# Up projection of the gated MLP as seven float16 block products per weight pair and 1,024 tokens, gated values through DRAM

## The chip, the cores and the metric

The kernel runs on one core of a Trainium2 chip. The core has TensorE (PE, matrix products out of SBUF into PSUM), VectorE (DVE), ScalarE (ACT) and GpSimd (POOL) for work by element, and SyncE (SP), which here only issues DMA transfers between DRAM and SBUF. The metric is the device time of one execution in microseconds. Each engine runs its own list of instructions in order; semaphores make one list wait for another.

## The reference

One layer of a diffusion block over 2,048 latent tokens of width 1,024 (and 256 context tokens, which only feed keys, values and states). First a mixer of attention and gated DeltaNet heads, then an output projection with a gated residual, then the part that is changed here:

```python
def conv_ffn(h, w_up, conv_w, conv_b, w_down):
    """Gated MLP with a centred depthwise conv between up-projection and activation."""
    u = depthwise_conv(h @ w_up, conv_w) + conv_b      # w_up (1024, 2*2816), conv over 3 tokens
    gate, val = jnp.split(u, 2, axis=-1)
    return (jax.nn.silu(gate) * val) @ w_down          # w_down (2816, 1024)
...
x = x + g1 * lat_out
x = x + g2 * conv_ffn(modulate(x, norm2_g[l], sh2, sc2), w_up[l], ffn_conv_w[l], ffn_conv_b[l], w_down[l])
return rms_norm(x, final_norm_g)
```

## The kernel before

Tokens lie along the free axis, features along the 128 partitions. D = 1024 makes KT = 8 tiles of 128 input features; the 2,816 hidden features make NJ = 22 pairs of a gate tile and a value tile; the 2,048 tokens make NCH = 4 blocks of 512.

The layer's earlier stages (projections, attention and the DeltaNet scan) and the output projection (`output`) are ordered by a list scheduler (`Plan`), which writes each engine's list from costs and priorities. All of the MLP behind it is issued in the order in which the code is written (`manual_schedule`).

Every product keeps about float32 accuracy by splitting each operand into a rounded part and the rest (float32r, "hi" and "lo") and adding three matmuls: hi by hi, hi by lo, lo by hi (`prods`, lines 520 to 522).

The MLP runs token block by token block. For each block there are 44 "up" units (one feature tile each, 8 x 3 = 24 matmuls of 128x512 into one PSUM bank `pu`), followed by 24 "down" units (8 output tiles `pdn`, each summed over 22 hidden tiles in parts of 8, 8 and 6). A unit's weights (`raw`, 2 buffers, 512 KB) are fetched by SP, rounded by ACT (`leading`, line 1703) and their rest taken by DVE (`rest`, line 1708) into `ws` (3 buffers), two units ahead; so up weights are loaded and split four times, once for each block. Behind an up unit `after_up` copies `pu` to SBUF (`ue`, line 1734), applies the three taps of the convolution on DVE (`cv`, lines 1742 and 1745), and after each value tile takes SiLU, multiplies, and splits the result into `hid`, which stays in SBUF: 22 tiles of hi and lo. Two tokens of each row are carried to the next block (`carry`).

The normalised input of the next block (`h2`) is read back from DRAM (`h2c`) and split while the down units run, one tile for each output tile (line 1842 ff.), and the final norm of a block (`last_norm`) is spread over the next block's up units.

Of the kernel before, what the change touches and what calls it, by code (L numbers as in the profile page):

```python
# [40 lines left out]
VTOP = 1024.0  # L41
GTOP, ROWV, SC = 2048.0, 4096.0, 1024.0
# [378 lines left out]
def kernel(  # L421
# [22 lines left out]
    h2c = dram.tile([NCH, P, KT, 512], F32, name="h2c")  # L444
    hcd = dram.tile([P, 2, KT, TC], F32, name="hcd")
# [1073 lines left out]
    hp3 = p3.enter_context(tc.tile_pool(name="hp3", bufs=1, side="right", reuse_waits="tile"))  # L1519

    def load_h2(pool, tag, bufs, tb):
        h2 = hp3.tile([P, 2, KT, 512], F32R, tag="h2", name=f"h2_{tb}")
        for k in range(KT):
            raw = pool.tile([P, 512], F32, tag=tag, name=f"h2raw_{tb}_{k}", bufs=bufs)
            SY.dma_start(out=raw, in_=h2c[tb, :, k, :])
            S.copy(out=h2[:, 0, k, :], in_=raw)
            V.tensor_tensor(out=h2[:, 1, k, :], in0=raw, in1=h2[:, 0, k, :].bitcast(F32), op=ALU.subtract)
        return h2

    def output(plan, x3, s3, ol3):  # L1530
# [50 lines left out]
        def normed(xv, tb):  # L1581
            acc = mk(s3, [P, 512], F32, "nacc", f"nacc_b{tb}", 2)
            S.activation(out=acc, in_=xv[:, 0, :], func=AF.Square)
            for k in range(1, KT):
# [3 lines left out]
            yield  # L1588
            ps = mk(psn, [P, 512], F32, "nps", f"nps_b{tb}", 1)
            for j in range(4):  # L1590
                PE.matmul(out=ps[:, 2 * j:2 * j + 2], lhsT=acc[:, j * P:(j + 1) * P], rhs=ones[:, 0:2], start=True,
                          stop=True)
            rs = rep_rstd(plan, psn, "nps", 1, s3, 2, ps, 512, f"b{tb}")
            for k in range(KT):
                V.scalar_tensor_tensor(out=xv[:, k, :], in0=xv[:, k, :], scalar=aff2[:, k:k + 1], in1=rs,
                                       op0=ALU.mult, op1=ALU.mult)
                S.activation(out=xv[:, k, :], in_=xv[:, k, :], func=AF.Identity, bias=mod2[:, 8 + k:9 + k])
                if k % 2:
                    SY.dma_start(out=h2_l[tb][:, k - 1:k + 1, :], in_=xv[:, k - 1:k + 1, :])
# [3 lines left out]
        h2 = None  # L1603
# [313 lines left out]
```

## Time and profile before

| | |
|---|---|
| median of 3 runs | 3490.8 us (3486.12 to 3490.93) |
| span of the profiled execution (no other time is given for it) | 3482.1 us |
| around the span, median less span | 8.7 us |
| MLP, from the first `pu` to the end | 3482.1 - 1995.6 = 1486.5 us |
| bytes from and to HBM, whole span | 306.17 and 88.11 MB |
| busy DVE, ACT and POOL, whole span | 66%, 48%, 41% |

The profile is one execution. A row of a group gives line, engine, operation, `out<-in` with shapes, count, busy us, mean ns of one, and then the time its engine sat idle before it and what ended that. A row of stages gives the busy time of each engine in a stretch of the span. In a timeline a row has start, duration, engine, line and names; an idle stretch before it stands in brackets with what ended it. PE rows overlap: a matmul of 512 columns is shown as 0.39 us long, while the next starts 0.23 us after it, so the pace is read from starts.

### The profile page before, as it was taken

The page shows a single profiled execution, that of the slowest core. Times are in us where ns is not written, and L with a number is a line of the kernel's source. Part 1 is how long each engine was busy: PE and PEld are TensorE (multiplying, and loading weights), DVE is VectorE, ACT ScalarE, POOL GpSimd, SP SyncE. Part 2 cuts the span into 40 slices and gives each one's busy share as a digit, 9 for nine tenths or more (in the row PEclk, how much of TensorE's full clock was granted, in tenths as well). Part 3 has the DMA queues.
Part 4 walks back from the last instruction along what each step waited for, and adds up shares of the span by engine and source line. Part 5 has one row for each costly group of instructions (what it writes and reads, how often), then busy time and mean ns, then how long its engine had stood idle before and what let it go on. Part 6 is the DMA issues. An engine that isn't in the chain of part 4 may idle for free.

```text
span 3482.1 us, 64968 instructions
## 1 busy us (share of the span) xinstructions
PE 3309.7 (95%) x26025; PEld 2692.3 (77%) x26025; DVE 2312.2 (66%) x3601; ACT 1661.9 (48%) x2600; POOL 1432.9 (41%) x1429
## 2 busy tenths in 40 slices
PE   6799999979999999999878999999999999999998
PEld 3799888857777777777556778888888888888898
DVE  5665577878777789888656577636773577447743
ACT  5443243457877777767644443323332333223331
POOL 5685455557777777778855411000110011001100
PEclk8899999999999999999989999999999999999999
DMA  6323335641222233222156733343334333433332
GB/s 232 88 66 96 123 114 147 190 136 56 79 86 92 67 110 91 90 88 74 41 176 211 241 119 97 101 135 103 116 96 133 110 117 96 123 118 116 97 108 92
DMA packets 218527, 398.09 MB, mean 114 GB/s; under 512 B 21496, under 2 KB 96856, under 8 KB 217952
## 3 DMA queue, kind: packets, MB, share of 16 engines
q1 hardware_dynamic: 216272, 388.52, 35.3%
q0 software_dynamic: 1952, 5.42, 0.6%
q8 instruction: 204, 3.34, 0.4%
q14 instruction: 99, 0.81, 0.1%
HBM read 306.17 MB, written 88.11 MB: 113 GB/s over the span
## 4 chain that ended last, share of the span: by engine, by line
PE 73%; DVE 10%; POOL 6%; DMA 4%; issue 3%; ACT 3%; SPq 0%; POOLq 0%; DVEq 0%; ACTq 0%
PE pu L521 9%; PE pu L522 9%; PE pu L520 9%; PE sc L403 6%; PE ops L403 5%; PE pdn L522 5%; PE pdn L521 5%; PE pdn L520 5%; PE po L403 3%; PE sm L403 2%; PE pa L403 1%; DVE mx L403 1%; PE pg L522 1%; PE pg L521 1%; PE pg L520 1%
## 5 line engine op out<-in xcount | busy, mean ns | idle before, releaser
L403 POOL TENSOR_TENSOR lp<-p,hp 128x1024 f16<-128x1024 f32 x288 | 623.3, 2172 | 212.2 <-DVE hp L403 66.9
L520 PE MATMUL pu<-h,ws_u 128*128 128x512 f32 x1408 | 550.8, 391 | 3.2 <-ACT h L403 3.2
L521 PE MATMUL pu<-h,ws_u 128*128 128x512 f32 x1408 | 549.3, 390 | 2.3 <-DVE h L403 2.3
L522 PE MATMUL pu<-h,ws_u 128*128 128x512 f32 x1408 | 548.9, 390 | 0.0
L1736 POOL COPY carry<-ue 128x2 f32<-128x2 f32 x132 | 25.2, 191 | 892.6 <-ACT ue L1734 892.6
L403 DVE TENSOR_REDUCE mx<-sm 128x1 f32<-128x512 f32 x512 | 336.6, 683 | 65.3 <-PE sm L403 63.7
L403 ACT ACTIVATE p<-sc 128x1024 f32<-128x1024 f32 x288 | 295.3, 1025 | 139.5 <-PE sc L403 128.2
L520 PEld LDWEIGHTS pu<-h,ws_u 128*128 128x128 f32 x1408 | 264.9, 188 | 60.2 <-ACT h L403 4.6
L521 PEld LDWEIGHTS pu<-h,ws_u 128*128 128x128 f32 x1408 | 264.9, 188 | 59.7 <-DVE h L403 4.0
L522 PE MATMUL pdn<-hid,ws_d 128*128 128x512 f32 (+2 forms) x880 | 307.4, 349 | 0.0
L521 PE MATMUL pdn<-hid,ws_d 128*128 128x512 f32 (+2 forms) x880 | 307.4, 349 | 0.0
L522 PEld LDWEIGHTS pu<-h,ws_u 128*128 128x128 f32 x1408 | 264.9, 188 | 54.6
L520 PE MATMUL pdn<-hid,ws_d 128*128 128x512 f32 (+2 forms) x880 | 306.4, 348 | 0.0
L1734 ACT COPY ue<-pu 128x512 f32<-128x512 f32 x176 | 103.4, 587 | 368.8 <-PE pu L522 367.4
L1745 DVE SCALAR_TENSOR_TENSOR cv<-ue,cols,cv 128x512 f32<-128x512 f32 (+1 forms) x352 | 265.0, 753 | 15.5
L1708 DVE TENSOR_TENSOR ws_u<-raw_u,ws_u 128x1024 fp32r<-128x1024 f32 x176 | 214.6, 1219 | 18.0 <-ACT ws_u L1703 18.0
L403 PE MATMUL sc<-q,kh 128*128 128x512 f16 x576 | 219.2, 381 | 4.9 <-ACT p L403 3.8
L1742 DVE TENSOR_SCALAR cv<-ue,cols 128x512 f32<-128x512 f32 (+1 forms) x176 | 96.4, 548 | 189.9 <-ACT ue L1734 185.4
L403 PE MATMUL sc<-qx,kx 128*128 128x512 f16 x576 | 219.1, 380 | 0.0
L1733 POOL COPY ue<-carry 128x2 f32<-128x2 f32 x176 | 95.6, 543 | 291.3 <-DVE cv L1745 291.2
L1708 DVE TENSOR_TENSOR ws_d<-raw_d,ws_d 128x1024 fp32r<-128x1024 f32 (+1 forms) x96 | 109.1, 1136 | 157.4 <-ACT ws_d L1703 155.2
L403 ACT CAST hp<-p 128x1024 f16<-128x1024 f32 x192 | 201.1, 1048 | 3.6
(586 smaller groups left out, 8070.5 us busy)
## 6 DMA issues: line engine op xcount, KB each, us to landing
raw_u<-in_wu SPq DMA_DIRECT2D x176, 512.0 KB
raw_d<-in_wd SPq DMA_DIRECT2D x64, 512.0 KB
tk<-gsc SPq DMA_DIRECT2D x34, 512.0 KB
tT<-gsc SPq DMA_DIRECT2D x66, 256.0 KB
wm<-in_wm SPq DMA_DIRECT2D x64, 256.0 KB
gsc<-kd SPq DMA_DIRECT2D x64, 256.0 KB
raw_o<-in_wo SPq DMA_DIRECT2D x32, 512.0 KB
raw_d<-in_wd SPq DMA_DIRECT2D x32, 384.0 KB
```

The source lines that it names most:

```text
L403: fn(**{k: v.get() if isinstance(v, Lazy) else v for k, v in kw.items()})
L520: PE.matmul(out=ps, lhsT=hi_l(k), rhs=hi_r(k), start=st, stop=False)
L521: PE.matmul(out=ps, lhsT=hi_l(k), rhs=lo_r(k), start=False, stop=False)
L522: PE.matmul(out=ps, lhsT=lo_l(k), rhs=hi_r(k), start=False, stop=en)
L1708: V.tensor_tensor(out=made[u][:, 1, :n], in0=raws[u][:, :n], in1=made[u][:, 0, :n].bitcast(F32), op=ALU.subtract)
L1733: G.tensor_copy(out=ue[:, 0:2], in_=carry[:, b, :])
L1734: S.copy(out=ue[:, 2:514], in_=ps)
L1736: G.tensor_copy(out=carry[:, b, :], in_=ue[:, 512:514])
L1742: V.tensor_scalar(out=cv[:, :W], in0=ue[:, 0:W], scalar1=fw[0], scalar2=cols[:, C_FB + b:C_FB + b + 1], op0=ALU.mult, op1=ALU.add)
L1745: V.scalar_tensor_tensor(out=cv[:, :W], in0=ue[:, i:i + W], scalar=fw[i], in1=cv[:, :W], op0=ALU.mult, op1=ALU.add)
```

## The change

**What is computed.** A pair (gate tile, value tile) of up weights is a 2 x 2 matrix of blocks: rows gate and value, columns the first and second 512 input features (A11, A12; A21, A22). The activations of 1,024 tokens are one too: rows the halves of the features, columns two token blocks (B11, B12; B21, B22). Their product has four results. Before, it takes eight block products of 4 x 3 = 12 matmuls each; the change takes seven (`P1` to `P7`, Strassen's scheme in Winograd's form) from sums of weights (S1 to S4) and of activations (T1 to T4), and adds the products up in PSUM and on DVE.

**Parts.** The parts are float16 (hi and lo, three matmuls as before) instead of float32r. So that they fit, activations are scaled by one bound from the modulation (`scale_h2`), weights by each pair's root mean square (`prep`: two ACT squares with accumulators, a small PE matmul `uns` that sums over partitions, a POOL power), and the convolution's taps are scaled back (`fw`).

**Order.** The up projection of all tokens now comes first, 22 pairs x 2 halves of the tokens = 44 steps; the weights of a pair are fetched and made once (`fetch_up`, `prep`: 7 ACT casts, 7 POOL subtractions, 4 DVE sums), spread over the two steps of the pair before. Each step works its own P1, P6, P5, P2, P7 and, between P6 and P5, the P4 and P3 of the step before. The blocks of the first 1,024 tokens are made inside the output projection (`early`), those of the second during the first steps (`late_blocks`), where the last token block's norm now also lies (`norm_tail`).

**Gated values** are written to DRAM (`hidc`) at the end of `after`, and the down units of each block read them back and split them (`load_part`, parts of 8, 8 and 6 tiles, through 3 buffers `hraw`; for the first block partly through 2 buffers inside the last up step). Parts 0 and 1 share the two buffers of `ol3`, part 2 has one; so part i of the next block can be filled only once part i of this one has been used for the last time. The final norm of a block (`last_norm`) now follows behind the next block's first down units.

```diff
+    hidc = dram.tile([NJ, P, T + 2], F32, name="hidc")
...
+    BLK = ("B11", "T2", "T1", "B21", "T3", "T4", "B22")
+    def split(hi_e, lo_e, dst, src):
...
+            hi_e.copy(out=dst[0], in_=src)
...
+        lo_e.tensor_tensor(out=dst[1], in0=src, in1=dst[0], op=ALU.subtract)
+    def prep(e, raw, j, junk_tag, s_tag):
+        g, v = raw
...
+        for r, t in enumerate((g, v)):
...
+            e.S.activation(out=junk, in_=t, func=AF.Square, accum_out=ss[:, r:r + 1])
+            yield
+        ps = e.tile(pt3, [P, 512], F32, "pt", f"uns_{j}", 2)
+        e.PE.matmul(out=ps[:, 0:2], lhsT=ones, rhs=ss, start=True, stop=True)
+        e.V.tensor_reduce(out=sg[:, 0:1], in_=ps[:, 0:2], axis=AX, op=ALU.add)
...
+        e.G.tensor_tensor(out=sg[:, 0:1], in0=sg[:, 0:1], in1=mhalf, op=ALU.pow)
+        yield
...
+        for t in (g, v):
+            e.S.activation(out=t, in_=t, func=AF.Copy, scale=sg[:, 0:1])
+            yield
...
+        def put(n, x):
+            split(e.S, e.G, [at[n][:, f] for f in range(2)], x)
+        e.V.tensor_tensor(out=s, in0=a21, in1=a22, op=ALU.add)
+        put("A11", a11)
+        yield
+        put("S1", s)
+        yield
+        e.V.tensor_tensor(out=s, in0=s, in1=a11, op=ALU.subtract)
+        e.V.tensor_tensor(out=a21, in0=a11, in1=a21, op=ALU.subtract)
+        put("S2", s)
...
+        e.V.tensor_tensor(out=a12, in0=a12, in1=s, op=ALU.subtract)
+        put("A22", a22)
+        yield
+        put("S4", a12)
+        yield
...
+        def product(ps, w, b, first):
+            for k in range(4):
+                for f, (x, y) in enumerate(((0, 0), (0, 1), (1, 0))):
+                    PE.matmul(out=ps, lhsT=w[:, x, k, :], rhs=b[:, y, k, :], start=first and k + f == 0,
+                              stop=k == 3 and f == 2, skip_group_check=True)
...
+        def P6(s):
+            s.bb = bank(s, "ub")
+            product(s.bb, s.w["S2"], s.b["T2"], True)
+            s.u2 = half(s, "u2", "nsq", 2)
+            V.tensor_tensor(out=s.u2, in0=s.bb, in1=s.s1, op=ALU.add)
...
+        def P7(s):
+            product(s.bb, s.w["S3"], s.b["T3"], False)
...
+            V.tensor_tensor(out=u3, in0=s.bb, in1=s.s1, op=ALU.add)
+            V.tensor_tensor(out=s.ev[:, 514:1026], in0=s.c, in1=u3, op=ALU.add)
+        def P4(s):
+            product(s.bb, s.w["A22"], s.b["T4"], False)
+            V.tensor_tensor(out=s.ev[:, 2:514], in0=s.bb, in1=s.s1, op=ALU.add)
...
+        def after(s):
+            W, cv = s.W, []
+            for r, t in enumerate((s.eg, s.ev)):
...
+                S.activation(out=c, in_=t[:, 0:W], func=AF.Identity, scale=s.fw[:, 3 * r:3 * r + 1],
+                             bias=cols[:, C_FB + b:C_FB + b + 1])
+                for i in (1, 2):
+                    V.scalar_tensor_tensor(out=c, in0=t[:, i:i + W], scalar=s.fw[:, 3 * r + i:3 * r + i + 1],
+                                           in1=c, op0=ALU.mult, op1=ALU.add)
...
+                yield
+            S.activation(out=cv[0], in_=cv[0], func=AF.Silu)
+            V.tensor_tensor(out=cv[1], in0=cv[0], in1=cv[1], op=ALU.mult)
+            SY.dma_start(out=hidc[s.j, :, 1024 * s.sb:1024 * s.sb + W], in_=cv[1])
+            yield
...
-        units += [("u", tb, b, 0, KT) for b in range(2 * NJ)]
-        units += [("d", tb, cb, a, n) for cb in range(KT) for a, n in parts]
+    units = [(tb, cb, a, n) for tb in range(NCH) for cb in range(KT) for a, n in parts]
...
+        def prepared(j):
+            yield from prep(direct, raw_u.pop(j), j, "nacc", "nacc")
+            if j + 1 < NJ:
+                raw_u[j + 1] = fetch_up(direct, j + 1)
...
+            elif sb == 0 and n >= 4 and j + 1 < NJ:
+                work = prepared(j + 1)
+            if final:
+                work = chained(load_part(0, 0, ol3.tile([P, 2, KT, OLW], F32R, tag="ol", name="hid_0_0"), s3, "ndg", 2))
+            for i, f in enumerate((P1, P6, P4, P3, P5, P2, P7)):
+                if f in (P4, P3):
+                    if prev:
+                        f(prev)
+                        if f is P3:
+                            post = after(prev)
+                else:
+                    f(s)
+                next(post, None)
...
+                next(extra, None)
+                next(work, None)
...
+    def load_part(tb, i, at, pool, tag, bufs):
...
+            SY.dma_start(out=raw, in_=hidc[a + k, :, 512 * tb:512 * tb + W])
+            S.copy(out=at[:, 0, k, :W], in_=raw)
+            (G if k % 3 == 2 else V).tensor_tensor(out=at[:, 1, k, :W], in0=raw, in1=at[:, 0, k, :W].bitcast(F32),
+                                                   op=ALU.subtract)
+            yield
...
+            for _ in range(6):
+                next(loads, None)
...
+            next(pend, None)
+            if b == KT - 1:
+                loads = chained(loads, load_part(tb + 1, i_part, part_tile(tb + 1, i_part), s4, "hraw", 3))
```

SP's list in the middle of the up stage. Before, it held nothing but weight fetches (`raw_u0_7` is token block 0, unit 7):

```order
L1697 DMA raw_u0_7_0_29852<-in_wu 128x1024
L1697 DMA raw_u0_8_0_29890<-in_wu 128x1024
L1697 DMA raw_u0_9_0_29933<-in_wu 128x1024
L1697 DMA raw_u0_10_0_29971<-in_wu 128x1024
L1697 DMA raw_u0_11_0_30014<-in_wu 128x1024
```

Now, around the steps of pair 5 (`cv_5_0_1` is the gated value tile of pair 5, first half of the tokens; `raw_u7_0` and `raw_u7_1` are the gate and value weights of pair 7):

```order
L1907 DMA hidc_71<-cv_4_1_1_31266 128x1026
L1907 DMA hidc_71<-cv_5_0_1_31397 128x1024
L1630 DMA raw_u7_0_31422<-in_wu 128x1024
L1630 DMA raw_u7_1_31423<-in_wu 128x1024
L1907 DMA hidc_71<-cv_5_1_1_31531 128x1026
L1907 DMA hidc_71<-cv_6_0_1_31662 128x1024
L1630 DMA raw_u8_0_31687<-in_wu 128x1024
```

Each pair's fetch now stands behind a write of gated values.

PE's list where one up unit meets the next, before:

```order
L521 MATMUL pu_1_1_32269<-h2_1_31518,ws_u1_1_0_32202 128x512
L522 MATMUL pu_1_1_32269<-h2_1_31518,ws_u1_1_0_32202 128x512
L520 MATMUL pu_1_2_32312<-h2_1_31518,ws_u1_2_0_32226 128x512
L521 MATMUL pu_1_2_32312<-h2_1_31518,ws_u1_2_0_32226 128x512
L522 MATMUL pu_1_2_32312<-h2_1_31518,ws_u1_2_0_32226 128x512
```

Now, in the first step of pair 7, between P4 and P3 of the step before (`ub_6_1`, `uc_6_1`: pair 6, second half):

```order
L1829 LDWEIGHTS ws_u6_1_31289
L1829 MATMUL ub_6_1_31596<-xb_29933,ws_u6_1_31289 128x512
L1588 MATMUL uns_8_31758<-uss_8_31723,k32_76 128x2
L1829 LDWEIGHTS ws_u6_1_31289
L1829 MATMUL uc_6_1_31649<-xa_29796,ws_u6_1_31289 128x512
```

The sum of pair 8's squares now stands in PE's list, third product in, one step after that pair's fetch in SP's list.

SP's list where token block 0 ends, before (`raw_d0_7_16`: last part of the last output tile; `x1p`: the residual):

```order
L1697 DMA raw_d0_7_16_32083<-in_wd 128x768
L1842 DMA h2raw_1_6_32109<-h2c_70 128x512
L1697 DMA raw_u1_0_0_32116<-in_wu 128x1024
L1697 DMA raw_u1_1_0_32140<-in_wu 128x1024
L1814 DMA x1p_0_7_32143<-x1c_69 128x512
```

Now, at the end of token block 1 (the fetch is for the next block's first output tile; `hraw_2_0` to `hraw_2_6` are hidden tiles of token block 2):

```order
L1791 DMA raw_d2_0_16_37267<-in_wd 128x768
L1814 DMA hraw_2_0_37269<-hidc_71 128x512
L1814 DMA hraw_2_1_37273<-hidc_71 128x512
L1814 DMA hraw_2_2_37277<-hidc_71 128x512
L1814 DMA hraw_2_3_37281<-hidc_71 128x512
L1814 DMA hraw_2_4_37285<-hidc_71 128x512
L1814 DMA hraw_2_5_37289<-hidc_71 128x512
L1791 DMA raw_d2_1_0_37321<-in_wd 128x1024
L1814 DMA hraw_2_6_37323<-hidc_71 128x512
```

Where one read of the next block's input stood among the weight fetches of each output tile, 22 reads of gated values now stand together between two token blocks.

More of the change, by code (lines that the diff above doesn't have):

```diff
@@ L41 @@
 VTOP = 1024.0
+HTOP, WTOP = 8192.0, 16384.0
 GTOP, ROWV, SC = 2048.0, 4096.0, 1024.0
@@ L1532, in output, with fetch_up @@
+    def fetch_up(e, j):
+        t = [e.tile(w3, [P, 2, 4, P], F32, "raw", f"raw_u{j}_{r}", RAWB) for r in range(2)]
+        for r in range(2):
+            e.SY.dma_start(out=t[r].rearrange("p a k f -> p (a k) f"), in_=wu[2 * j + r])
+        return t
+    up_w = {}
+    def output(plan, x3, s3):
         V, S, G, PE, SY = plan.V, plan.S, plan.G, plan.PE, plan.SY
@@ L1579, in weights, with squares @@
             return ws
[L1581 to L1584, printed above, removed]
+        def squares(xv, tb, acc, k):
+            if k == 0:
+                S.activation(out=acc, in_=xv[:, 0, :], func=AF.Square)
+            else:
                 sq = mk(s3, [P, 512], F32, "nsq", f"nsq_b{tb}_{k}", 2)
@@ new lines, in output @@
+                if end and 2 <= cb < 6:
+                    early(cb - 2)
+            if end:
+                for _ in prep(plan, fetch_up(plan, 0), 0, "nsq", "osq"):
+                    pass
+            pend = normed(xv, tb, acc)
+        at, fw = up_w[0]
+        plan.keep([xv, acc, at["A11"], at["S4"], fw, blk0["B11"]] + [blk0[m] for m in BLK[4:]])
+        plan.issue(dict(o=("work", 1.0)))
+        up_w[0] = {m: t.get() for m, t in at.items()}, fw.get()
+        return xv.get(), acc.get(), {m: t.get() for m, t in blk0.items()}
@@ new lines, in rest @@
+    def rest(u):
+        if u < len(units):
+            n = units[u][3]
+            V.tensor_tensor(out=made[u][:, 1, :n], in0=raws[u][:, :n], in1=made[u][:, 0, :n].bitcast(F32),
+                            op=ALU.subtract)
+            del raws[u]
+            fetch(u + 2)
+    def load_part(tb, i, at, pool, tag, bufs):
+        a, n = parts[i]
+        W = 514 if tb == NCH - 1 else 512
+        hids[tb, i] = at
+        for k in range(n):
+            raw = pool.tile([P, OLW], F32, tag=tag, name=f"hraw_{tb}_{a + k}", bufs=bufs)[:, :W]
+            SY.dma_start(out=raw, in_=hidc[a + k, :, 512 * tb:512 * tb + W])
+            S.copy(out=at[:, 0, k, :W], in_=raw)
+            (G if k % 3 == 2 else V).tensor_tensor(out=at[:, 1, k, :W], in0=raw, in1=at[:, 0, k, :W].bitcast(F32),
+                                                   op=ALU.subtract)
+            yield
@@ L1664 @@
+    with tc.manual_schedule():
+        direct = Direct(nc)
+        xv_, acc_, blk0 = output(Plan(tc, psn, pt3, ps3), x3, s3)
+        zc = w3.tile([P, KT], F32, name="zc", bufs=1)
         G.memset(zc, 0.0)
@@ L1758 @@
-    with tc.manual_schedule():
-        for u in range(2):
-            fetch(u)
-        for u in range(2):
-            leading(u)
-            rest(u)
-        post, pend = iter(()), None
-        for u, (how, tb, b, a, n) in enumerate(units):
+        finish(x2, tb, (0, 512), rs)
+        yield
+    with tc.manual_schedule():
+        loads = load_part(0, 2, part_tile(0, 2), s4, "hraw", 3)
+        post, pend = iter(()), iter(())
+        x2 = None
+        for u, (tb, b, a, n) in enumerate(units):
```

407 lines of the change are left out of this document (264 added, 143 removed).

## The prediction

> **What bounds the kernel now.** First the page: the whole span, and the chain of work that ended last by line. Then the stages of the MLP, one row each: the first row is the output projection, then up and down of each token block, and the tail.
>
> ```profile
> span 3482.1 us, 64968 instructions
> PE pu L521 9%; PE pu L522 9%; PE pu L520 9%; PE sc L403 6%; PE ops L403 5%; PE pdn L522 5%; PE pdn L521 5%; PE pdn L520 5%; PE po L403 3%; PE sm L403 2%; PE pa L403 1%; DVE mx L403 1%; PE pg L522 1%; PE pg L521 1%; PE pg L520 1%
> ...
> 1770.37:1995.64 225.27, 205.32 (x897) 160.50 (x896) 125.82 (x162) 95.28 (x149) 114.71 (x81) 0.97 0.61 210
> 1995.64:2247.15 251.51, 246.00 (x1068) 201.19 (x1066) 177.76 (x237) 102.67 (x146) 25.48 (x89) 0.99 0.35 109
> 2247.15:2369.45 122.30, 122.30 (x529) 99.15 (x528) 41.34 (x44) 29.32 (x35) 0.57 (x2) 1.00 0.41 130
> 2369.45:2611.41 241.96, 241.42 (x1067) 199.40 (x1066) 176.23 (x236) 95.10 (x137) 24.68 (x87) 1.00 0.33 105
> ...
> 2733.72:2975.69 241.97, 241.43 (x1068) 199.44 (x1066) 176.15 (x236) 95.05 (x137) 24.84 (x87) 1.00 0.33 104
> ...
> 3097.99:3340.05 242.06, 241.42 (x1067) 199.42 (x1066) 176.57 (x236) 95.20 (x137) 42.24 (x83) 1.00 0.33 104
> 3340.05:3467.44 127.39, 127.39 (x1065) 127.30 (x1063) 42.76 (x63) 28.51 (x40) 1.32 (x1) 1.00 0.32 97
> 3467.44:3482.10 14.66, 2.00 (x8) 1.02 (x6) 6.26 (x17) 0.42 (x1) 1.01 (x1) 0.64 0.40 144
> ```
>
> From up to down PE (first number behind the length) never rests: it is the bound, everything else is cover, and the four up stages take 251.5 + 242.0 + 242.0 + 242.1 = 977.5 us. The first is 9.5 us longer, since its input came late. Whatever makes PE wait in the new order is paid in full.
>
> **What the change removes.** The pace of matmuls is read from two starts, 32 rows apart for the float32r ones and four apart for float16 ones of the attention:
>
> ```profile
> 2239.67 0.39 PE L520 MATMUL pu<-h,ws_u 128*128 128x512 f32 x1
> ...
> 2246.92 0.39 PE L522 MATMUL pu<-h,ws_u 128*128 128x512 f32 x1
> ...
> 1478.06 0.38 PE L403 MATMUL sc<-q,kh 128*128 128x512 f16 x1
> ...
> 1478.92 0.59 PE L403 MATMUL sm<-kh,q 128*128 128x512 f16 x2
> ...
> 2000.31 0.99 PE L403 MATMUL nps_b<-k,nacc_b 128*128 128x2 f32 x8
> ```
>
> That is 0.2266 and 0.215 us. The order has 44 steps x 84 = 3,696 products where 4,224 stood: 3,696 x 0.215 = 794.6 us. The 22 sums `uns` are like a call of `nps` (eight rows for four calls: 0.25 us each): 5.5. So up falls from 977.5 to 800.1, **-177 us**. Weights are made once, not four times; nothing waited for that.
>
> **Wait 1: each pair's squares, +78.** These rows give the durations:
>
> ```profile
> L1745 DVE SCALAR_TENSOR_TENSOR cv<-ue,cols,cv 128x512 f32<-128x512 f32 x264 | 198.6, 752 | 9.3
> L1708 DVE TENSOR_TENSOR ws_u<-raw_u,ws_u 128x1024 fp32r<-128x1024 f32 x176 | 214.6, 1219 | 18.0 <-ACT ws_u L1703 18.0
> L1755 DVE TENSOR_TENSOR hid<-cv,hid 128x512 fp32r<-128x512 f32 x66 | 45.8, 694 | 45.4 <-ACT hid L1754 45.4
> L1703 ACT CAST ws_u<-raw_u 128x1024 fp32r<-128x1024 f32 x176 | 185.6, 1054 | 23.3 <-PE pdn L522 19.3 <-POOL carry L1685 2.3 <-DMA raw_u<-in_wu 1.8
> L403 ACT ACTIVATE x<-x,mod 128x512 f32<-128x512 f32 x24 | 15.8, 719 | 5.4 <-DVE x L403 5.2
> L403 ACT ACTIVATION_READ_ACCUMULATOR osq<-oraw 128x1 f32 x12 | 2.2, 186 | 0.0
> L403 POOL TENSOR_TENSOR lp<-p,hp 128x1024 f16<-128x1024 f32 x288 | 623.3, 2172 | 212.2 <-DVE hp L403 66.9 <-ACT hp L403 59.1 <-DVE vi L403 16.4
> L403 POOL TENSOR_TENSOR ll<-db,lh 128x512 f16<-128x512 f32 x36 | 47.9, 1331 | 12.3 <-ACT lh L403 12.3
> ...
> 1867.18 2.72 POOL L403 TENSOR_TENSOR ws_o<-raw_o,ws_o 128x1024 fp32r<-128x1024 f32 x1 [0.27 <-ACT ws_o L403]
> 1867.61 2.83 DVE L403 TENSOR_TENSOR oraw<-oraw,oss 128x512 f32<-128x512 f32 x1
> ...
> 1913.67 0.68 DVE L403 TENSOR_TENSOR oraw<-oraw,oss 128x512 f32<-128x512 f32 x1
> ...
> 1876.27 5.46 DMA raw_o<-in_wo
> ...
> 1924.03 9.51 DMA raw_o<-in_wo
> ...
> 1937.16 3.54 DMA raw_o<-in_wo
> ```
>
> A step is 7 x 2.58 = 18.06 us of PE. In a pair's second step P3 of the step before ends at 10.3. Behind it, in order: DVE's sum 0.69; ACT's first tap 1.15 (719 ns, and 434 more for twice the width, as the casts of both widths differ); four taps on DVE at 1.28 (752, and 530 more); `prep`'s subtraction 0.69; the gating product 1.22; some 0.6 of semaphores. That makes 19.8. Two of `prep`'s POOL subtractions fall between the taps. The two rows at 1867 show what follows: a DVE sum that takes 0.68 alone takes 2.83 beside a POOL subtraction; so each puts DVE off by up to 1.33, and I take 2.4 for both. The product ends at 22.2, 4.1 us into the next step. Only then does SP issue its write, and behind that the fetches of the next pair but one: the value rows go out at 4.9, third of three transfers of 512 KB. I take 5.46 for it, a weight load behind other loads: 10.4. ACT squares them (1.05 + 0.19 + 0.2): 11.8. PE reaches `uns` behind its third product, at 7.7, and P3, P5, P2 and P7 stand behind it. **4.1 us, 19 times** (pairs 3 to 21): 78. With no blocking by POOL and the 3.54 landing, `uns` is ready at 7.5 and costs nothing; with 9.51 it is 8.2 x 19 = 155.
>
> The Trainium skill, SBUF — State Buffer, "Who interferes with whom", has a rule against this change: a DVE instruction with two SBUF inputs and a GpSimd instruction that reads SBUF exclude each other for their whole length. The pair of rows at 1867 agrees with it (2.83 against 0.68 us). Without such a lock the wait would be 1.7 us x 19 = 32, and the sum below 46 us less.
>
> **Waits 2 to 4: loads where none were.** The rows of a read of the next input, its cast and its subtraction, and of a norm:
>
> ```profile
> 2255.64 0.44 SPq L1842 DMA_DIRECT2D h2raw<-h2c  x1
> 2259.07 0.62 ACT L1843 CAST h<-h2raw 128x512 fp32r<-128x512 f32 x1 [5.08 <-DMA h2raw<-h2c]
> 2259.72 0.69 DVE L1844 TENSOR_TENSOR h<-h2raw,h 128x512 fp32r<-128x512 f32 x1 [4.48 <-ACT h L1843]
> ...
> 2444.55 1.65 POOL nrc_f L479
> 2446.22 0.89 DVE ndg_f L484 x4
> 2447.24 1.10 PE nrs_f L486 x2
> ```
>
> *Between token blocks, +60.* From issue to cast 3.4 us, cast 0.62, subtraction 0.69, gaps 0.3: a buffer turns in 5.0. Part 0 is free when the last output tile has used it. Three tiles are then ready after 2.1 us; the other 19 of 22 need seven turns of three buffers: 37. In PE's list the norm's `nrs` stands ahead of the third down unit, and its POOL power behind the last POOL subtraction of the loads: 37 + 1.65 + 0.89 + 1.1 = 41, then 18 matmuls at 0.2316 (122.3 us / 528) = 4.2: 45. PE's own work in that stretch is 108 x 0.2316 = 25. So 20 us, three times. If the norm is not in the way 12, if transfers slow down by one us per turn 27.
>
> *From up to down, +38.* In the last step two buffers and four turns of 5 us carry part 0, between DVE's own sums; P4 waits for `u3` some 15 us. Part 1 then takes four turns (20), behind it stand the last step's taps (4 x 1.28 + 2 x 1.15 + 1.22 = 8.6), its write (3.5) and part 2's two turns (9): 41 against the 15.3 of PE's first output tile, less the first tiles' lead, 23 more. Bounds 15 and 50.
>
> *Start, +31.* Blocks of the second half need token block 3: its norm, a write, a read, and with three buffers two more rounds, in which the taps' own write lies: six transfers in series at 3.5 = 21, 14 casts at 1.05, eight POOL subtractions of the double width at 2.17, taps 8.6. T2 of the second half is ready some 70 us after the first product; PE wants it after two steps and a product, 38.7. Bounds 15 and 45.
>
> *Output projection, +4:* it gains 28 casts, 32 DVE and 12 POOL operations in a stage where ACT is busy 95 and DVE 126 of 225 us; mostly hidden, bounds -5 and 12. Down's matmuls and the tail stay.
>
> **Sum.** -177 + 78 + 60 + 38 + 31 + 4 = **+34** on the span of 3482.1; around it lie 8.7 us up to the median of 3490.8. Forecast **3525 us**, slower by 1.0%; its own range is 3490 to 3560.
>
> **Rivals.**
> 1. *The weights come in time* (not slower). Place: the fetch behind the gating write. Price: 78, hence 3447. It decides when the value rows land by 6.3 us into the step (7.7 less 1.44). For it: DMA is busy 0.33 in the up stages. Against: three transfers at once, and DVE's list.
> 2. *Loads overlap better* (20 to 8, 38 to 18, 31 to 15): 72 less, 3453. For it: the reads need no semaphore but a free buffer. Against: three buffers only.
> 3. *The clock drops at each wait.* These rows follow waits of up to 2.6 us:
>
> ```profile
> 2003.85 0.80 PE L520 MATMUL pu<-h,ws_u 128*128 128x512 f32 x1 [2.55 <-ACT h L403]
> ...
> 2005.60 0.63 PE L520 MATMUL pu<-h,ws_u 128*128 128x512 f32 x1
> 2006.03 0.63 PE L521 MATMUL pu<-h,ws_u 128*128 128x512 f32 x1
> ...
> 2013.72 0.54 PE L520 MATMUL pu<-h,ws_u 128*128 128x512 f32 x1
> ```
>
> Matmuls come 0.43 apart, for some 16 of them. At each of 19 waits that is 16 x 0.215 = 3.4 us, 65 in all: 3590. Against it: that stretch held several waits. The Trainium skill, TensorE: Matmul & The Clock Gate, Part 1, gives the rule: half clock after an idle window of about 3.4 us, until a busy one. The trace agrees on the half, and shows it after a wait of 2.55 us, with others ahead of it.
> 4. *It doesn't do what it says:* the seven products keep the old pace of 0.2266: 3,696 x 0.0116 = 43 more, 3568.
>
> **Chances.** Forecast 0.52, the rivals 0.18, 0.14, 0.11, 0.05. The range 3430 to 3595 takes in all of them and both bounds of the smaller terms. Measurements here tell 0.2% (7 us) from no change. Faster: rivals 1 and 2, 0.32. Within 0.2%: the low edge of the forecast's own range, 0.06. Slower: the rest, 0.62.
>
> **What would show it.** Right: up matmuls 0.215 apart; PE idle before `uns` about 19 times, behind ACT, some 4 us each; idle between down stages of about 20 us; down stages of 142 us in place of 122. Wrong: an up stage with `uns` not waited for; DVE sums as PE's releaser in every step, which would make DVE the bound; down stages near 122.

## The result, and the profile after

The changed kernel takes 3629.24 us (median of 4 runs, 3628.26 to 3634.78) where the kernel before takes 3490.77 (3486.12 to 3490.93): ratio 1.0409, 95% interval 1.0394 to 1.0423. It is slower, as forecast, but by 4.1% and not 1.0%: 3525 was said, and 3629 lies above the whole range.

A span is 1.8 us shorter than the time of its execution (3633.0 against 3634.78), so most of the 8.7 us that the prediction put around the span were a difference between two executions. The profiled execution of the changed kernel was the slowest of its four, and the one of the kernel before, 3482.1 + 1.8 us, lies below its three timed ones; so the spans differ by 150.9 us where the medians differ by 138.5, and the difference of a stage read from these two profiles holds to some 12 us.

The page of the changed kernel: the span, and the chain of work that ended last, by line.

```profile
span 3633.0 us, 63480 instructions
...
PE uc L1829 6%; PE sc L404 6%; PE ub L1829 5%; PE ops L404 5%; DVE cv L1899 4%; PE pdn L522 4%; PE pdn L524 4%; PE pdn L523 4%; PE po L404 4%; DMA hraw<-hidc 3%; DMA raw_u<-in_wu 3%; PE ua L1829 3%; PE sm L404 2%; PE pa L404 1%; DVE mx L404 1%
```

In the same list of before, all rows of the MLP were PE's. Now three things stand in it that are no matmuls: DVE's taps (`cv`), the reads of the hidden rows (`hraw`) and the fetch of weights (`raw_u`).

The stages, one row each, from the first `po` on: output projection, up, down (with the last two products of up, 5.2 us). Behind the length stands PE's busy time, at the end of the row the granted clock, the DMA share and GB/s.

```profile
1774.90:2048.10 273.20, 218.85 (x897) 169.33 (x896) 164.54 (x197) 113.68 (x183) 130.71 (x95) 0.91 0.54 187
2048.10:2999.60 951.50, 855.03 (x3723) 376.77 (x3724) 552.19 (x608) 387.51 (x521) 294.22 (x377) 0.93 0.17 57
2999.60:3618.20 618.60, 536.87 (x2704) 446.57 (x2703) 232.12 (x290) 164.17 (x224) 37.65 (x33) 0.93 0.44 133
```

Length less busy is the time in which PE waits. Busy less the work at full pace is taken here as what slow matmuls cost: in up 3,672 products at 0.215 us and 5.5 for `uns`, 795.0; in down the 494.3 of before and 5.2; in the output projection the 205.3 of before. In us:

| stage | forecast | measured | waits forecast | waits | lost to slow matmuls |
|---|---|---|---|---|---|
| output projection | 229.3 | 273.2, and starts 4.5 later | 24 | 54.4 | 13.6 |
| up | 909.1 | 956.7 | 109 | 96.5 | 60.0 |
| down | 592.3 | 613.4 | 98 | 81.7 | 37.4 |

On the profiled spans 116.9 us are missing (3633.0 against 3482.1 + 34; on the medians 104.4). The last column makes 111 of them: PE was not only waiting, it also ran slower behind its waits, and the granted clock of the three stages is 0.91, 0.93 and 0.93 where the kernel before had 0.97 in the first and 0.99 to 1.00 in the others. The waits come out 6 us above forecast in sum: the output projection 35 above (with its later start), the other two 29 below.

The longest waits of PE: who waited for whom, us in total, times, longest.

```profile
PE uns L1588 <- ACT junk L1585: 66.6, 21, 3.5
PE pto L404 <- DVE oraw L404: 37.9, 17, 4.7
PE nrs_f L488 <- DVE ndg_f L486: 29.4, 3, 11.1
PE nps_f L506 <- DVE nacc_f L498: 22.3, 3, 8.3
PE pdn L522 <- ACT hid L1815: 20.7, 8, 11.4
```

`uns` is wait 1 of the prediction; `nrs_f`, `nps_f` and `pdn` are the waits around the down stages; `pto` is the output projection's.

One `uns` in the changed kernel's timeline (start, length, and in brackets the idle time ahead). PE:

```profile
2597.74 0.38 PE L1588 MATMUL uns<-uss,k 128*128 128x2 f32 x2 [3.01 <-ACT junk L1585]
2597.99 4.44 PE L1829 MATMUL uc<-xa,ws_u 128*128 128x512 f16 x12
2602.22 2.79 PE L1829 MATMUL uc<-blk,ws_u 128*128 128x512 f16 x12
```

SP's list at the same place, with the gating write first:

```profile
2590.01 0.33 SPq L1907 DMA_DIRECT2D hidc<-cv  x1
2590.43 1.21 SPq L1630 DMA_DIRECT2D raw_u<-in_wu  x2
```

And ACT, which squares the rows:

```profile
2595.25 1.06 ACT L1585 ACTIVATE junk<-raw_u 128x1024 bf16<-128x1024 f32 x1 [5.07 <-DMA raw_u<-in_wu]
```

The order is the forecast one: SP sends the fetch right behind the gating write, ACT waits 5.07 us for the rows, PE waits 3.01 us. Then twelve products take 4.23 us (2597.99 to 2602.22) where twelve otherwise take 2.59. Three windows, cut where the granted clock changes (it is the third number from the end, PE's busy time the second):

```profile
2595.45:2598.87 3.42, 1.13 (x7) 0.65 (x8) 0.17 (x2) 2.10 (x4) 0.37 (x2) 1.00 0.10 40
2598.87:2602.28 3.41, 3.41 (x10) 1.21 (x9) 0.00 (x0) 0.00 (x0) 0.36 (x1) 0.50 0.00 0
2602.28:2605.69 3.41, 3.41 (x17) 1.53 (x16) 1.72 (x2) 2.37 (x3) 0.00 (x0) 1.00 0.00 0
```

The slow products lie in one stretch of 3.41 us at half the clock, which begins 1.1 us behind the end of the wait.

### The profile page after: what moved, and what is told of

It is laid out like the page before. It is cut to its first block, busy times and chain, and to the rows that moved or that the text cites. A ratio compares the mean times of both kernels' runs of the same rounds, so it can differ in the third digit from the quotient of the medians.

```text
span 3633.0 us, 63480 instructions
## 1 busy us (share of the span) xinstructions
PE 3252.4 (90%) x25544; PEld 2300.8 (63%) x25544; DVE 2264.1 (62%) x3403; ACT 1727.6 (48%) x2676; POOL 1656.3 (46%) x1494
## 4 chain that ended last, share of the span: by engine, by line
PE 57%; DVE 17%; DMA 11%; POOL 6%; ACT 5%; issue 3%; SPq 1%; POOLq 0%; ACTq 0%; DVEq 0%
PE uc L1829 6%; PE sc L404 6%; PE ub L1829 5%; PE ops L404 5%; DVE cv L1899 4%; PE pdn L522 4%; PE pdn L524 4%; PE pdn L523 4%; PE po L404 4%; DMA hraw<-hidc 3%; DMA raw_u<-in_wu 3%; PE ua L1829 3%; PE sm L404 2%; PE pa L404 1%; DVE mx L404 1%
## 5 line engine op out<-in xcount | busy, mean ns | idle before, releaser
L1829 PEld LDWEIGHTS <-ws_u 128*128 128x128 f16 x3696 | 374.3, 102 | 504.2 <-issue 82.4
L522 PE MATMUL pdn<-hid,ws_d 128*128 128x512 f32 (+2 forms) x880 | 319.0, 363 | 20.8 <-ACT hid L1815 20.7
L1899 DVE SCALAR_TENSOR_TENSOR cv<-xa,ufw,cv 128x1024 f32<-128x1024 f32 (+1 forms) x176 | 258.9, 1472 | 66.5 <-ACT cv L1896 63.3
L1829 PE MATMUL ua<-blk,ws_u 128*128 128x512 f16 x1056 | 246.1, 383 | 13.2 <-ACT blk L1574 7.5
L404 PE MATMUL po<-ol,ws_o 128*128 128x512 f32 x768 | 201.1, 422 | 15.1 <-ACT ws_o L404 9.0
L1577 POOL TENSOR_TENSOR ws_u<-raw_u,ws_u 128x512 f16<-128x512 f32 x105 | 143.4, 1374 | 149.0 <-ACT ws_u L1574 149.0
L1896 ACT ACTIVATE cv<-xa,cols,ufw 128x1024 f32<-128x1024 f32 (+1 forms) x88 | 108.6, 1238 | 206.6 <-DVE xa L1887 201.8
L522 PEld LDWEIGHTS pdn<-hid,ws_d 128*128 128x128 f32 x880 | 170.6, 194 | 50.9 <-ACT hid L1815 25.8
L404 PE MATMUL ops<-vst,hp 128*128 128x65 f16 (+1 forms) x4608 | 192.5, 194 | 7.0 <-DVE hp L404 3.3
L523 PEld LDWEIGHTS pdn<-hid,ws_d 128*128 128x128 f32 x880 | 170.5, 194 | 36.2 <-DVE hid L1816 7.4
L404 PEld LDWEIGHTS po<-ol,ws_o 128*128 128x128 f32 x768 | 154.3, 204 | 55.9 <-ACT ws_o L404 9.4
L404 PEld LDWEIGHTS <-hp 128*128 128x128 f16 x4608 | 170.6, 98 | 24.1 <-DVE hp L404 5.0
L524 PEld LDWEIGHTS pdn<-hid,ws_d 128*128 128x128 f32 x880 | 170.3, 194 | 23.4
```

The costliest lines, as they stand in the source:

```text
L404: fn(**{k: v.get() if isinstance(v, Lazy) else v for k, v in kw.items()})
L522: PE.matmul(out=ps, lhsT=hi_l(k), rhs=hi_r(k), start=st, stop=False)
L523: PE.matmul(out=ps, lhsT=hi_l(k), rhs=lo_r(k), start=False, stop=False)
L524: PE.matmul(out=ps, lhsT=lo_l(k), rhs=hi_r(k), start=False, stop=en)
L1577: lo_e.tensor_tensor(out=dst[1], in0=src, in1=dst[0], op=ALU.subtract)
L1829: PE.matmul(out=ps, lhsT=w[:, x, k, :], rhs=b[:, y, k, :], start=first and k + f == 0, stop=k == 3 and f == 2, skip_group_check=True)
```

## The experiments

### e1: the fetch ahead of the gating write

```diff
 def prepared(j):
-    yield from prep(direct, raw_u.pop(j), j, "nacc", "nacc")
-    if j + 1 < NJ:
-        raw_u[j + 1] = fetch_up(direct, j + 1)
+    raw, more = raw_u.pop(j), j + 1 < NJ
+    nv = one(j + 1, 1) if more else None        # value half: third buffer
+    yield from prep(direct, raw, j, "nacc", "nacc", ahead)
...
         put("A22", a22)
+        if ahead:
+            ahead()                             # raw_u[j + 1] = (one(j + 1, 0), nv)
```

Fetches and squares also take the value half first.

> The changed kernel waits 66.6 us (21 times) before uns in its up stage of 951.5 us, at a granted clock of 0.93. Theory A, the fetch of the next pair stands in SP's list behind the gating write: with the value half fetched before the pair is prepared and the gate half as soon as A22's parts are made, ahead of that write, these waits fall below 10 us and the up stage to 880 to 895 us, the time by about 60 us to some 3570. Theory C, as A, and the waits are also what lowers the clock: the up stage falls further, to 840 to 870 us, with a granted clock of 0.97 or more. Rival B, the squares are late because of ACT's own list or the landing of three transfers at once, not because of the order in SP's list: more than 40 us of waits before uns stay, and the up stage is above 930 us.

Measured: 3530.62 us (3527.35 to 3532.28), ratio to before 1.0111 [1.0095, 1.0128], 98.6 below the changed kernel. Two windows of e1, the up stage and its steady part:

```profile
2043.10:2896.30 853.20, 812.76 (x3723) 367.54 (x3724) 550.14 (x608) 382.88 (x521) 295.30 (x377) 0.97 0.19 64
...
2200.00:2840.00 640.00, 640.00 (x2992) 293.00 (x2991) 430.33 (x476) 296.15 (x406) 221.79 (x299) 1.00 0.17 58
```

What is left of the wait in e1:

```profile
PE uns L1588 <- ACT junk L1585: 9.6, 2, 6.2
```

The waits fall by 57 us, the stage by 98.3: theory C, within its numbers. PE's idle time fell by 56 (96.5 to 40.4), its busy time by 42 with the same instructions. In the steady part PE is busy without a gap at a clock of 1.00.

### e8: the waits kept, PE kept busy in them

```diff
+        if j > 2:
+            wm = psn.tile([P, 512], F32, tag="nps", name=f"warm_{j}", bufs=1)
+            for _ in range(14):
+                e.PE.matmul(out=wm, lhsT=up_w[j - 1][0]["A11"][:, 0, 0, :], rhs=warm[0][:, 0, 0, :], start=True, stop=True)
         ps = e.tile(pt3, [P, 512], F32, "pt", f"uns_{j}", 2)
```

> The changed kernel with 14 products ahead of uns from pair 3 on, whose results nobody reads: they fill the 3.0 us in which PE waits for the squares, 14 x 0.215 us. Theory C, a wait of 3 us makes the clock drop afterwards: after such a wait the next 12 products take 4.23 us in place of 2.58, some 1.7 us each time; with PE kept busy that goes, 19 to 21 times: the up stage falls from 951.5 by 25 to 36 us at a granted clock of 0.96 or more, the time to about 3598 us. Rival M, the slow products behind a wait have another cause (their operands, the memory): the stage stays within 6 us, and the time within 8 us of 3629. If the products outlast the wait they add at most 0.5 us each time, 10 us.

Measured: 3595.56 us (3593.95 to 3603.7), ratio 1.0306 [1.029, 1.0322], 33.7 below the changed kernel. The up stage of e8:

```profile
2045.90:2966.40 920.50, 875.23 (x3989) 392.38 (x3990) 551.88 (x608) 386.88 (x521) 295.42 (x377) 0.97 0.18 59
```

PE in e8 at one place where the filler stands:

```profile
2577.51 3.19 PE L1590 MATMUL warm<-blk,ws_u 128*128 128x512 f16 x14
2580.96 0.38 PE L1592 MATMUL uns<-uss,k 128*128 128x2 f32 x2 [0.27 <-ACT junk L1585]
2581.20 2.75 PE L1833 MATMUL uc<-xa,ws_u 128*128 128x512 f16 x12
2583.79 2.75 PE L1833 MATMUL uc<-blk,ws_u 128*128 128x512 f16 x12
```

The twelve products behind `uns` take 2.59 us again. Nothing but idleness was taken away, `uns` comes as late as before, and the stage is 31 us shorter: theory C. That separates the two parts of e1: of its 98, some 57 were the wait itself and some 40 the pace behind it.

### e7: nothing of POOL beside DVE's taps

```diff
 def put(n, x):
-    split(e.S, e.G, [at[n][:, f] for f in range(2)], x)
+    if j:
+        e.S.copy(out=at[n][:, 0], in_=x)
+        e.G.memset(at[n][:, 1], 0.0)
+    else:
+        split(e.S, e.G, [at[n][:, f] for f in range(2)], x)
```

The kernel leaves out the low parts of the up weights from pair 1 on; POOL writes zeros in their place and reads nothing.

> The changed kernel with POOL's subtractions of the up weights (their low parts, from pair 1 on) left out: POOL only sets the low parts to zero, so nothing of POOL reads SBUF beside DVE's taps. In the trace two taps that start beside such a subtraction take 3.38 us in place of 2.61, twice in a step, and the gating product comes 1.6 us later. Theory L, the prediction's: this delay is part of the wait for uns, which is 3.0 us each; without it 20 waits get 1.6 us shorter, from 66.6 to 30 to 40 us, and the up stage falls from 951.5 by 30 to 55 us, the clock's part included. Rival, the delay on DVE has cover and other steps of the chain set when the write goes out: the waits stay above 55 us, the stage above 935 us.

Measured: 3567.82 us (3566.4 to 3569.35), ratio 1.0228 [1.0214, 1.0242], 61.4 below the changed kernel. DVE's taps between 2100 and 2900 us, grouped by line (behind the busy time stands the mean of one in ns), in the changed kernel:

```profile
L1899 DVE SCALAR_TENSOR_TENSOR cv<-xa,ufw,cv 128x1024 f32<-128x1024 f32 (+1 forms) x149 | 221.3, 1485 | 59.5 <-ACT cv L1896 56.9
```

The same group in e7:

```profile
L1903 DVE SCALAR_TENSOR_TENSOR cv<-xa,ufw,cv 128x1024 f32<-128x1024 f32 (+1 forms) x164 | 211.0, 1287 | 64.0 <-ACT cv L1900 61.1
```

The up stage of e7:

```profile
2050.40:2935.80 885.40, 822.08 (x3724) 367.24 (x3725) 503.65 (x608) 388.79 (x521) 172.24 (x377) 0.97 0.18 61
```

PE's wait in e7, in total:

```profile
PE uns L1588 <- ACT junk L1585: 35.5, 21, 5.2
```

And one such wait in PE's timeline:

```profile
2564.98 0.38 PE L1588 MATMUL uns<-uss,k 128*128 128x2 f32 x2 [1.34 <-ACT junk L1585]
2565.22 2.75 PE L1833 MATMUL uc<-xa,ws_u 128*128 128x512 f16 x12
2567.81 2.54 PE L1833 MATMUL uc<-blk,ws_u 128*128 128x512 f16 x11
```

Theory L. The wait falls to 35.5 us, as said; the stage falls by 66, beyond the 30 to 55. Half of that is idle time (96.5 to 63.3), half is pace (855.0 to 822.1 busy), more than I had counted: behind a wait of 1.34 us the twelve products take 2.59 us. In the steady part the waits are 1.3 to 2.3 us long, and 18 of 19 cost only their length.

That POOL's reads hold a buffer of `raw_u` back, which e7 would also have removed, is not the cause: between 2100 and 2900 us of the changed kernel SP waits 736.1 us for `cv` and never for a buffer of the weights.

### e4: eight buffers for the rows that are read back

```diff
-        loads = load_part(0, 2, part_tile(0, 2), s4, "hraw", 3)
+        loads = load_part(0, 2, part_tile(0, 2), s4, "hraw", 8)
```

The loads of the later token blocks have the same edit.

> Eight buffers in place of three for the hidden rows that are read back. Theory T (the prediction's term for the passages): a turn of a buffer of about 5 us, three at a time, sets when the next token block's rows are ready; with eight the waits of PE for nps_f, nrs_f and hid (75 us in 14) fall by 30 us or more, and the down stages from 618.6 to about 590 us or less. Rival K: the casts on ACT and the subtractions on DVE and POOL, in the order in which they stand among the weights' own, set it; the waits fall by less than 10 us and the stage stays above 608 us.

### e3: the norm behind the second output tile's units

```diff
-    h4p = p3.enter_context(tc.tile_pool(name="h4p", bufs=1, side="right", reuse_waits="tile"))
+    h4p = p3.enter_context(tc.tile_pool(name="h4p", bufs=2, side="right", reuse_waits="tile"))
...
-            next(pend, None)
+            if b:
+                next(pend, None)
```

The loop that runs the rest of the norm is put under the same condition.

> In the changed kernel's down stages (618.6 us with the last two products of up) PE waits 22.3 us for nps_f and 29.4 us for nrs_f at the three passages between token blocks. Here the norm of a finished block is put behind the units of the second output tile, with a second buffer for its rows. Theory N, the norm in PE's list is the wait: both waits fall below 8 us together and the stage falls by 35 to 50 us. Rival L, the reads of the next hidden rows are late in any case and the norm only stands where PE would wait anyway: waits of pdn for hid grow from about 24 to over 55 us and the stage falls by less than 15 us.

Measured: e4 3592.46 us (3589.79 to 3593.89), ratio 1.0289 [1.0274, 1.0305]; e3 3620.73 (3614.85 to 3626.58), ratio 1.0371 [1.0354, 1.0389]. The down stage of e4:

```profile
3003.30:3575.40 572.10, 526.79 (x2703) 439.71 (x2702) 234.72 (x290) 163.37 (x224) 39.02 (x33) 0.95 0.47 143
```

PE's waits in it:

```profile
PE pdn L522 <- ACT hid L1815: 17.8, 6, 11.8
PE nrs_f L488 <- DVE ndg_f L486: 15.4, 3, 6.6
PE nps_f L506 <- DVE nacc_f L498: 5.0, 3, 2.0
```

The down stage of e3:

```profile
3004.80:3609.60 604.80, 547.98 (x2703) 445.87 (x2702) 232.57 (x290) 164.03 (x224) 38.76 (x33) 0.94 0.46 136
```

And PE's waits of e3:

```profile
PE pdn L522 <- ACT hid L1815: 36.8, 25, 12.3
PE pdn L523 <- POOL hid L1816: 7.4, 10, 0.9
PE pdn L523 <- DVE hid L1816: 6.4, 16, 1.1
...
PE nrs_f L488 <- DVE ndg_f L486: 2.3, 3, 0.8
```

e4 is theory T: the three waits fall from 72.4 to 38.2 us, the stage by 46.5, the median of the whole kernel by 36.8. e3 is nearer to rival L: of the norm's 51.7 us 2.3 are left, but `pdn` waits 36.8 us for ACT's parts in place of 20.7, and 13.8 for the subtractions, and the stage gains only 14: its waits together fall by 25 us (81.7 to 56.8), but PE's busy time rises by 11 (536.9 to 548.0). PE's busy time at half the clock is 53.9 us in place of 51.0, so little of that rise is the clock's; what the rest is, no run takes apart. So the ring of three buffers was the limit between token blocks, and the norm mostly stood where PE would have waited for rows.

### e2 and e11: why the transposes of the output projection were late

e2 puts the squares of the first three token blocks back into one run, and the two steps of their norm back behind the second and the fourth output tile, where the kernel before has them; e11 is the kernel before with the changed kernel's ring of three buffers (`"oraw", ..., 4` becomes 3).

```diff
 def normed(xv, tb, acc):
+    if tb != order[-1]:
+        for k in range(KT):
+            squares(xv, tb, acc, k)
+    yield
     yield from norm_tail(plan, xv, tb, acc, s3, h2_l[tb])
...
-                squares(xv, tb, acc, cb)
+                if end:
+                    squares(xv, tb, acc, cb)
```

> The changed kernel's output projection takes 273.2 us against 225.3 before. Theory S, the squares that now stand in each output tile's own list put the square of the mixed rows (osg, on ACT) behind a square that waits for PE's current tile, and so every transpose (pto) comes late: with the squares of the first three token blocks put back into one run behind their block, the waits of PE for oraw fall from 37.9 to about 21 us and the stage by 15 to 25 us. Rival R, the ring of three buffers for the mixed rows in place of four makes the transposes late: the waits stay at 33 or more and the stage within 6 us of 273. Rival E, nearly all the loss is the blocks and the first pair's weights made in the last quarter: the stage falls by less than 8 us although the waits fall.

> The kernel before with three buffers in place of four for the rows mixed in the output projection, as the change has it. Theory S (e2), the ring costs nothing, the place of the squares did: the stage stays at 225 us within 3 and the time within 5 us of before. Rival R, the ring delays the transposes: the stage is 6 us longer or more.

Measured: e2 3611.06 us (3608.32 to 3619.6), ratio 1.0348 [1.0331, 1.0364]; e11 3489.98 (3485.4 to 3498.0), ratio 1.0001 [0.9991, 1.0011]. ACT in the changed kernel ahead of one transpose:

```profile
1880.09 0.63 ACT L404 ACTIVATE nsq_b<-x 128x512 f32<-128x512 f32 x1 [4.02 <-DVE x L404]
1880.63 0.62 ACT L404 ACTIVATE osg<-oraw 128x512 f32<-128x512 f32 x1
```

PE at that transpose:

```profile
1887.16 1.23 PE L404 MATMUL pto<-k,oraw 128*128 128x128 f32 x8 [2.41 <-DVE oraw L404]
```

The output projection of e2:

```profile
1776.20:2026.90 250.70, 207.40 (x897) 161.47 (x896) 158.28 (x197) 114.90 (x183) 136.73 (x95) 0.94 0.59 204
```

And what is left of the wait in e2:

```profile
PE pto L404 <- DVE oraw L404: 20.8, 13, 4.7
```

The square of the mixed rows (`osg`) stands on ACT behind a square of the current output tile (`nsq_b`), which waits 4.02 us for a sum on DVE that waits for PE (5.73 us, for `po`); the mixed rows, and PE's next transposes, come that much later. With the squares and the norm's steps elsewhere the wait is 20.8 in place of 37.9 us and the stage 22.5 shorter (18.2 by the medians): theory S, though e2 doesn't part the squares from the norm's steps. In the kernel before the ring costs nothing, as e11's row shows:

```profile
1773.70:2000.30 226.60, 207.24 (x896) 162.11 (x896) 126.03 (x162) 95.52 (x149) 115.12 (x81) 0.97 0.61 209
```

### e5 and e6: all of it together, and the last output weights made earlier

e5 holds e1 to e4 (five buffers for the rows). e6 adds:

```diff
-                if wts:
+                for _ in range(min(len(wts), 2 if end and cb == 0 else 1)):
                     ready.append(weights(*wts.pop(0)))
```

> The four edits of e1 to e4 in one kernel, with five buffers for the hidden rows, since the second buffer of the norm's rows leaves no room for eight. Theory A, the four terms are separate: against the changed kernel's 3629 us e1 gave 99, e2 18, e4 37 and e3 8.5; with five buffers I take 38 for the last two together: 155 less, 3474 us, 0.5% below the kernel before. Theory B, waits also lower the clock elsewhere, so taking them all away gives more than the sum: 3445 us or less. Rival, the loads and the norm share one cover, and the up stage's start moves with the output projection: less than 130 in all, 3500 us or more.

> As e5, and in the last token block of the output projection the weights are made two output tiles ahead, so that on ACT the casts of the last weights stand ahead of the 28 casts of the early blocks. In e2 PE waits 11.5 us for such a cast and some 4 us for POOL's halves behind it, and 11.5 us more before the first product of up. Theory O, the place in ACT's list is the price: PE's waits for ws_o fall below 3 us and the time is 9 to 16 us below e5's. Rival W, the blocks' casts and sums are the limit and the wait moves to the first products of up: within 4 us of e5.

Measured: e5 3473.73 us (3469.11 to 3482.33), ratio 0.9961 [0.9948, 0.9974]; e6 3467.76 (3464.5 to 3468.54), ratio 0.9939 [0.9927, 0.9952]. e5 hits theory A (3474): the terms add up, and pace came with each of them already. e6 gives 6 us, between its two theories: the wait for the cast moved, in part, to the first pair's squares. The wait in e6:

```profile
PE uns L404 <- ACT junk L404: 20.0, 1, 20.0
```

DVE has no gap in the first 25 us of that stretch (from 2000.39 to 2025.66 us), and the same operation of the blocks (`blk_B`) takes 1.64 us at 2003.55 and 0.68 at 2007.27.

### e9 and e10: the early blocks, and the first pair ahead of them

```diff
 def early(k):
+    for m in BLK:
+        plan.add("G", lambda out: tc.nc.gpsimd.memset(out, 0.0), "memset", dict(out=blk0[m][:, :, k, :]))
+    return
```

```diff
-            if end:
-                for _ in prep(plan, fetch_up(plan, 0), 0, "nsq", "osq"):
-                    pass
+                if end and cb == 3:             # inside the loop over cb
+                    for _ in prep(plan, fetch_up(plan, 0), 0, "nsq", "osq"):
+                        pass
```

Both stand on e6. e9 leaves out the blocks of the first 1,024 tokens, their reads, casts and sums, and multiplies zeros in their place.

> e6 with the early blocks of the first half left out: no reads, no casts, no sums, their tiles are set to zero by POOL. In e6 the output projection takes 251.0 us up to the first product of up (225.3 before), of which PE waits 20.0 us for the first pair's squares, and DVE works without a pause from 2000 to 2029 us of the span on these blocks, its operations at 1.64 us where one beside POOL's takes longer than the usual 0.68. Theory B, the blocks' work on DVE and ACT, done in the last quarter, is what is left of the loss there: without it the wait for the squares falls below 6 us and the stage to 230 to 238 us. Rival F, the first pair's own chain (its fetch behind the last output weights, squares, power, scaling, casts) is the limit: the wait stays above 12 us, the stage above 242 us. The first products of up lose their waits for blocks either way, as far as these blocks go.

> e6 with the first pair's weights made behind the second of the four early blocks' rows in place of behind all, so that its squares, sum, scaling and casts have two output tiles as cover. Theory G, in e6 the pair's serial chain (from its squares at 2019 to the first product at 2030.8) stands behind DVE's list of blocks and has no cover: the wait of 20.0 us for uns goes, PE then waits for the blocks, some 10 us less in the output projection, 3456 to 3462 us. Rival D, DVE's list is the limit and its length does not change: within 4 us of e6's 3468. Rival P, the pair's casts delay the last output weights: slower than e6.

Measured: e9 3456.34 us (3452.05 to 3463.45); e10 3473.75 (3469.36 to 3477.79), ratio 0.9951 [0.9938, 0.9963]. The output projection of e9:

```profile
1782.40:2017.90 235.50, 206.50 (x898) 162.68 (x898) 139.06 (x165) 99.19 (x155) 132.48 (x104) 0.96 0.59 199
```

The output projection of e10:

```profile
1778.00:2041.40 263.40, 211.65 (x897) 163.94 (x896) 170.34 (x198) 117.85 (x187) 144.03 (x103) 0.90 0.56 192
```

And PE's longest wait in it:

```profile
2019.78 1.22 PE L404 MATMUL po<-ol,ws_o 128*128 128x512 f32 x2 [28.35 <-ACT ws_o L404]
```

Theory B: without the blocks' work the stage is 235.5 us in place of e6's 251.0, the median 11.4 lower. e10 missed: the wait for `uns` went, a wait of 28.35 us for an output weight took its place, and it is 6 us slower than e6, as its rival P had it. This other order does not hide the work; whether DVE's time or the places in the lists are what is short in this quarter, these runs don't tell apart.

## Why the prediction was wrong

**Matmuls, -177: right.** In the steady part the products come 0.216 apart (twelve in 2.59 us), in e1 and e6 without a gap. Rival 4 is out.

**Wait 1, +78: right in mechanism, 18 us too long.** The 19 waits of the steady part are 60 us, each 3.2 where 4.1 was said; two more at the start make it 66.6. Its two causes held: the place in SP's list (e1) and the delay of DVE by POOL (e7: the taps' mean falls from 1485 to 1287 ns; 46 us were named as its worth, the waits fell by 31, and the pace behind them gave 33 more). The rule of the Trainium skill, SBUF — State Buffer, "Who interferes with whom", that was weighed there agrees with e7.

**Rival 3, the clock: this is the step that failed.** I set it beside the forecast as another case, with 0.11, and let every wait cost its length. It belonged in the sum. e8 shows it: 14 products that nobody reads, no other change, 34 us less. Each of the 19 steady waits costs about 2 us more than its length, where the rival had 3.4: behind 14 of them the clock is half for one stretch of 3.41 us, which loses 1.7, behind 5 for two, and the rival's 16 products at 0.43 are two. But the clock fell in all three stages, not only behind these 19 waits: of PE's busy time 37.7, 104.5 and 51.0 us lie in stretches at half the clock (9.3 us in the output projection of the kernel before). Half of what was added, 92 us, is lost to the clock, most of the miss; the other 19 of the 111 are not explained by it. By experiment this is tested in up; in the other two stages it rests on the granted clock. My argument against the rival, that the quoted stretch held several waits, did not hold: one wait is enough.

**Output projection, +4: the term of the sum that was most mis-sized, 48 us.** Some 5 of them are no work of the change: in e11, which takes as long as the kernel before, the stage also starts 3.3 us later than in the profile of before and takes 1.3 longer. I counted operations against free time on ACT and DVE and called them hidden. What matters is in which list, behind what: 22.5 us were squares ahead of the mixed rows (e2), 15.5 the early blocks' work in the last quarter (e9 against e6). The rest, about 10, is not taken apart; PE's waits there for the last output weights (14.8 us, 1.0 before) and for the first pair's squares (5.0) lie in it, and the second hangs on the early blocks: it is 20.0 us in e6 and 3.6 in e9.

**Between token blocks, +60, and up to down, +38: 98 forecast, 81.7 waited.** Between blocks PE waits 54 us (16 to 19 at each passage, 20 said), from up to down 28. The ring of three was the limit as said (e4). That `nps_f` would wait too, 22.3 us behind the last square, I had not seen, but it took the place of waits that I had counted for rows (e3). At the end of up, P4 waited 3.6 us for `u3` where 15 was said.

**Start, +31: the size came out, in part by luck.** The terms that were named for the 70 us (21, 14 casts at 1.05, eight subtractions at 2.17, taps 8.6) add up to 62, which would have made 23 of the 31. The waits of up other than `uns` are 30 us (96.5 less 66.6). The longest of them:

```profile
PE ub L1829 <- ACT ws_u L1574: 9.1, 2, 7.6
PE ua L1829 <- ACT blk L1574: 7.5, 1, 7.5
```

The blocks of the second half (`blk`) and token block 3's norm (`nrs_b`, 3.7 us) make about half of the 30; the weights of the first pairs (`ws_u`), of which I had not thought, make 13.

**Rival 1** (the weights come in time) is e1: I gave it 78 us, it is worth 99, since the pace comes with the wait. **Rival 2** (loads overlap better) is out: its 24, 18 and 15 us were 54, 28 and 30.

With the waits that were a matter of order and of buffers reduced (e6), the change does gain: 0.6%, 95% interval 0.5 to 0.7%, of the 5% that the fewer products hold.

## What to carry to other kernels

On a PE-bound kernel like this one count a wait of some 3 us as 5, and one of 1.5 us as itself: give each wait two columns, its length and the pace behind it, and look at the granted clock of that stage. For work that is to be hidden ask in which engine's list it stands and what waits behind it; the share of busy time says nothing of that. And a fetch that nobody waits for yet belongs ahead of a write that waits for a long chain (a queue of its own was not tried here).

## What the runs showed of the hardware

In the traces the granted clock changes only at points that lie a multiple of 3.41 us apart, and it is either full or half. A wait of 3.01 us left PE busy for 1.13 us of such a step, and the next step ran at 0.50. The length of a wait alone does not decide: in e7 one of 1.74 us was followed by a half step and one of 2.27 us was not. The idle time within one step says more. In the 13 traces, from 2000 us on, every one of the 208 full steps in which PE was idle for 2.0 us or more was followed by a half step; of some 4,700 with at most 1 us, none was; between 1 and 2 us both happen. The wait of 1.74 us lay within one step:

```profile
2446.56:2449.98 3.42, 1.68 (x10) 0.72 (x8) 0.85 (x2) 2.30 (x4) 0.22 (x2) 1.00 0.09 35
2449.98:2453.39 3.41, 3.41 (x10) 1.19 (x9) 0.00 (x0) 0.00 (x0) 0.52 (x1) 0.50 0.00 0
```

The one of 2.27 us, from 2868.55 to 2870.82, spread over two steps.

The Trainium skill, TensorE: Matmul & The Clock Gate, Part 1, speaks of idle windows of about 3.4 us that run freely. The traces agree on the length, but a window need not be idle as a whole: 2.0 us in it were enough, and here the measured number decides.

In e8, 14 filler products in each gap of the steady part were worth 34 us, although nobody reads their results.
